# Two of eight tiles of the merged tensor, and two of 22 of the down projection's input, stored 64 bytes further up in a two-layer encoder kernel

## The chip, the core and the metric

The kernel runs on one core of a Trainium2 chip. The metric is the device time of one execution in microseconds. Before the change three runs took 911.18, 912.65 and 914.66 us; their median, 912.65 us, is the time before.

## What is computed

Two layers on a sequence of 256 tokens with 1024 features, all in float32, then a final norm. Each layer is

```python
h = rmsnorm(x);  p = h @ w_in                     # 1024 x 6672
o_dn = gated_delta_rule(...both directions)       # 512 features
o_hg = hgrn2_scan(...both directions)             # 512 features
merged = sigmoid(g_dn) * (o_dn @ w_branch_dn) + sigmoid(g_hg) * (o_hg @ w_branch_hg)
x = x + merged @ w_out                            # 1024 x 1024
h = rmsnorm(x);  gate, up = split(h @ w_up)       # 1024 x 2 * 2816
x = x + (silu(dwconv(gate) + bias) * up) @ w_down # 2816 x 1024
```

The change concerns `merged`, the input of `w_out`, and the input of `w_down`.

## The kernel before

Features lie on the 128 partitions, tokens along the free axis, so an activation of 1024 features is eight tiles of 128 x 256 (`KT = 8`, `T = 256`), and the down projection's input is 22 (`NF`). A large product is made from two roundings to `float32r`: a high part and the remainder, of the weights (`wh`, `wl`, made at L217 and L218 from a 128 x 1024 piece of raw weights that SP's queue has loaded) and of the activations (`xh`/`xl`, `mhi`/`mlo`, `hh`/`hl`, made by `split_act`, L278 to L281). For each 128 x 128 block of weights and each tile `k` of the activation TensorE does three products into one PSUM tile: `wh` with the high part, `wh` with the low part, `wl` with the high part (`Gemm.run`, all recorded at L149). The weights are the stationary operand, loaded anew for every product; the activation tile, 256 columns, is the moving one. A product is named in the profile by output, moving operand, stationary operand: `ps<-mhi,wh`. In a few of the input projections (`tokens=True`) the roles are turned: there the weights move and the activation is stationary (`ps<-wh,xh`).

A column pair is 256 output features, two PSUM halves (`m`). So per column pair there are 3 products x 2 halves x the number of tiles: 48 for eight tiles, 132 for 22.

The end of a layer, the part that matters here, goes in this order:

- `branches` (L940): the two branch products; their sum, gated, is split tile by tile into `mhi` and `mlo`, eight tiles of 256 columns each, kept in one tile of SBUF apiece.
- `project`: four column pairs with `w_out`, 4 x 48 = 192 products. The last tiles, `k` = 6 and 7, come out of `branches` last, and the scheduler lets some products of the second column pair go ahead of them.
- `ffn` (L1000 on): 22 column pairs with `w_up`, 22 x 48 = 1056 products on `xh`/`xl`; each gives one tile `j` of the down projection's input, split into `hh` and `hl` (tags `h0`, `l0`, `h1`, ...), each its own SBUF tile.
- then four column pairs with `w_down`, 4 x 132 = 528 products over `j` = 0 to 21. In the first layer products for the next layer (`ps<-xw,early`) stand between them, in the second, at the start of the third and the fourth column pair, three transposes (`pt`, L1129).

The order on every engine is set by the framework's scheduler, from the order of the calls and the priorities in `OPT["order"]`. Nothing in the second half of the layer is looped at run time.

Where tiles lie is partly chosen by hand. `placed` pads a tile by 64 elements (256 bytes) and starts it `shift` elements in:

```python
t_ = pool.tile([P, n + 64], dtype, **kw)[:, shift:shift + n]
```

In the built program every moving operand of the float32r products whose weights are stationary (`ohl`, `mhi`, `mlo`, `xh`, `xl`, `hh`, `hl`, `sas`) starts 192 bytes above a multiple of 256, and every stationary block of weights at a multiple of 256. In the turned products it is the reverse: moving at 0, stationary at 192. This text calls the remainder modulo 256 bytes an operand's **phase**.

Of the kernel before, what the change touches and what calls it, by code (L numbers as in the profile page):

```python
# [11 lines left out]
F32R = mybir.dt.float32r  # L12
# [5 lines left out]
P = 128  # L18
T = 256
D = 1024  # L20
KT = 8
# [6 lines left out]
OPT = {  # L28
    "f32": ((1, 4, 5, 6, 14), (1, 4, 5, 6, 14)),
    "hb": 1,  # L30
    "pad": 2,
    "obb": 2,
    "kcb": 2,
    "ahead": 2000,
    "raw": 3,
    "w": 3,
# [82 lines left out]
def trunk(ctx: ExitStack, tc: tile.TileContext, x_in, consts, masks, vec, rows, w16, w_in, w_br, w_out, w_up, w_down, out):  # L119
# [46 lines left out]
    for c in range(4):  # L166
        t_ = xp.tile([P, 2 * T + 2], F32, tag=f"x{c}", name=f"x{c}")
# [20 lines left out]
    def placed(pool, dtype, shape, shift, **kw):  # L188


        n = math.prod(shape)
        t_ = pool.tile([P, n + 64], dtype, **kw)[:, shift:shift + n]
        if len(shape) == 2:
            return t_.rearrange("p (a b) -> p a b", a=shape[0])
        return t_.rearrange("p (a b c) -> p a b c", a=shape[0], b=shape[1])

    def tmp(name, tag="tmp"):
        return tp.tile([P, 512], F32, tag=tag, name=name, bufs=OPT[tag])
# [6 lines left out]
    def split_piece(src, n):  # L205
        with tc.high_priority(offset=OPT["ahead"]):
            return split_piece_(src, n)
# [51 lines left out]
    def gemm(src, xh, xl, nk=KT, tokens=False, tail=0, parts=None):  # L259
        return Gemm(src, xh, xl, nk, tokens, tail, parts).run()  # L260
# [17 lines left out]
    def split_act(src, hi, lo):  # L278
        act.copy(hi, src)
        dve.tensor_tensor(lo, src, hi.bitcast(F32), ALU.subtract)  # L280
        return hi, lo  # L281
# [117 lines left out]
    def mixer(l, pre, rs):  # L399
        V = vecs[:, l]  # L400
        with ExitStack() as mc:
            mp = mc.enter_context(tc.tile_pool(name=f"mp{l}", bufs=1, reuse_waits=OPT["rw"]))
# [46 lines left out]
            for k0 in range(0, KT, 4):  # L449
# [3 lines left out]
                hi = xp.tile([P, 4, T], F32R, tag=f"xh{k0}", name="xh")  # L453
                lo = xp.tile([P, 4, T], F32R, tag=f"xl{k0}", name="xl")
# [8 lines left out]
            cb = mp.tile([P, 2, 8, P], F32, tag="cb", name="cb")  # L463
# [47 lines left out]
            qk = mp.tile([P, 2, H, T], F32, tag="qk", name="qk")  # L511
# [386 lines left out]
            hl = {}  # L898
# [41 lines left out]
            def branches():  # L940
                oh = [hl[i][0][:, h] for i in range(2) for h in range(H)]
                ol = [hl[i][1][:, h] for i in range(2) for h in range(H)]
                mhi = placed(mp, F32R, (KT, T), OPT["at"][l][1], tag="qk", name="mhi")
                mlo = placed(mp, F32R, (KT, T), OPT["at"][l][1], tag="cb", name="mlo")
                for c in range(4):
                    pb = [pg.tile([P, 512], F32, tag="g", name="pbr") for _ in range(2)]
                    gs = [Group(24) for _ in range(2)]
                    for i in range(2):
                        wh, wl = split_piece(w_br[l, c, i], 1024)
                        for kk in range(4):  # L950
                            a, b_ = oh[4 * i + kk], ol[4 * i + kk]
                            for m in range(2):
                                o = pb[m][:, i * T:(i + 1) * T]
                                whm, wlm = wh[:, kk, m * P:(m + 1) * P], wl[:, kk, m * P:(m + 1) * P]
                                gs[m].mm(o, whm, a)
                                gs[m].mm(o, whm, b_)
                                gs[m].mm(o, wlm, a)
                    for m in range(2):
                        tm = tmp("mg")
                        dve.tensor_tensor(tm, pb[m], sgs[0][:, 2 * c + m].rearrange("p a b -> p (a b)"), ALU.mult)  # L960
                        dve.tensor_tensor(tm[:, 0:T], tm[:, 0:T], tm[:, T:512], ALU.add)
                        a, b_ = split_act(tm[:, 0:T], mhi[:, 2 * c + m], mlo[:, 2 * c + m])
                        mh.append(a)
                        ml.append(b_)

# [2 lines left out]
            def project():  # L968
                rs, xs = Rms(), SplitX(V[:, V_FFN:V_FFN + 8])
                up = Gemm(lambda i: w_up[l, 0, i], xs.h, xs.l)  # L970
                for c in range(4):
                    if c == 3 and OPT["eu"]:
# [7 lines left out]
            stages = {"gs": gatesums, "k0": lambda: conv(2), "k1": lambda: conv(3),  # L980
                      "ks": kstats, "qs": qstats, "vt": vtok, "de": decay, "gn": lambda: gram(0), "gp": lambda: gram(1), "so": solve, "in": inverse,
                      "dl": delta, "do": dnout, "br": branches, "pr": project}
            for i, c in enumerate((0, 1, 4, 5)):
                stages[("q0", "q1", "v0", "v1")[i]] = lambda c=c: conv(c)
# [17 lines left out]
    def ffn(l, rs, xs, first):  # L1002
        V = vecs[:, l]
        last = l == OPT["layers"] - 1
        with tc.tile_pool(name=f"fp{l}", bufs=1, reuse_waits=OPT["rw"]) as fp:

            def early(src):
                t_ = fp.tile([P, 1024], F32, tag="early", name="early", bufs=2 * len(PRE))
                sp.dma_start(t_, src)
                return t_  # L1010

            hh, hl = [], []
            for j in range(NF):
                ps = gemm(lambda i: w_up[l, j, i], xs.h, xs.l) if j else first.run()
                if j == 0:
                    rb = rs.spread(fp)
                pad = fp.tile([P, T + 2], F32, tag="fpad", name="fpad", bufs=3)
                pool.memset(pad[:, 0:1], 0.0)
                pool.memset(pad[:, T + 1:T + 2], 0.0)
                dve.tensor_tensor(pad[:, 1:T + 1], ps[:, 0:T], rb, ALU.mult)  # L1020
                up = fp.tile([P, T], F32, tag="up", name="up", bufs=3)
                dve.tensor_tensor(up, ps[:, T:512], rb, ALU.mult)
                w = V[:, V_FCONV + 3 * j:V_FCONV + 3 * j + 3]
                cv = fp.tile([P, T], F32, tag="cv", name="cv", bufs=3)
                act.activation(cv, pad[:, 0:T], AF.Identity, scale=w[:, 0:1], bias=V[:, V_FBIAS + j:V_FBIAS + j + 1])
                for i in (1, 2):
                    dve.scalar_tensor_tensor(cv, pad[:, i:i + T], w[:, i:i + 1], cv, op0=ALU.mult, op1=ALU.add)  # L1027
                sl = fp.tile([P, T], F32, tag="sl", name="sl", bufs=3)
                act.activation(sl, cv, AF.Silu)
                dve.tensor_tensor(up, up, sl, ALU.mult)  # L1030
                hi = fp.tile([P, T], F32R, tag=f"h{j}", name="hh")
                lo = fp.tile([P, T], F32R, tag=f"l{j}", name="hl")
                a, b = split_act(up, hi, lo)
                hh.append(a)
                hl.append(b)
            rs = Rms()
            pre = None if last else Pre(l + 1, early)
            for c in range(4):
                if c == 3 and not last:
                    with tc.high_priority(offset=OPT["ep"]):  # L1040
                        todo = pre_order(6)
                        pre.mm(todo[:OPT["ek"]])
                if c == OPT["ec"] and not last:
                    pre.ahead(l + 1)
                gm = Gemm(lambda i: w_down[l, c, i] if i < 5 else w_down[l, c, i][:, 0:512], hh, hl, NF,
                          tail=OPT["mt"] if c == 3 else 0)
                ps = gm.run()
                parts = 2 if c == 3 and OPT["mt"] else 1
                for i in range(0, 2, 2 // parts):
                    s = slice(i, i + 2 // parts)  # L1050
                    dve.tensor_tensor(xx2[c][:, s], xx2[c][:, s], ps.rearrange("p (a b) -> p a b", a=2)[:, s], ALU.add)
                if not last:
                    pre.add(c)
                rs.add(c, parts)
                if last:
                    for k in (2 * c, 2 * c + 1):
                        act.activation(x[k], x[k], AF.Identity, scale=V[:, V_FIN + k:V_FIN + k + 1])
            if not last:
                if OPT["pc"]:
                    pre.last = gm.g.prev  # L1060
                rest = todo[OPT["ek"]:] + [(j, k) for j in range(len(PRE)) for k in (6, 7)]
                rs, _ = meet(pre, rs, rest, OPT["fa"])
        return pre, rs

    def pre_order(n):
        return [(j, k) for j in range(len(PRE)) for k in range(n)]

    def meet(pre, rs, todo, n):

        pre.mm(todo[:n])  # L1070
        rm, rs = rs, rs.finish(pre.last if n else None)
        pre.mm(todo[n:], rm.last)
        return rs, rm
# [62 lines left out]
    for i in range(4):  # L1136
        h, b = divmod(i, 2)
        o = op.tile([P, 4 * P], F32, tag="o", name="o")
# [85 lines left out]
```

## Time and profile before

| what | value |
|---|---|
| runs before | 911.18, 912.65, 914.66 us, median 912.65 |
| the profiled execution | 911.13 us |
| its span, first to last instruction | 909.0 us |
| TensorE busy (PE) | 888.8 us, 98% of the span |
| weight loads (PEld) | 869.6 us, 96% |
| VectorE (DVE), ScalarE (ACT) | 670.6 us (74%), 559.5 us (62%) |
| mean granted TensorE clock | 0.993 |

The profiled execution took 2.1 us more than its span, for what lies around it. Busy time of PE is a union of overlapping products: one product is recorded as some 280 ns long while the next starts within 120 ns. How fast the engine goes is therefore read from the distance between the starts of neighbouring products, and from how many fall into a stretch. In a table of stretches the number behind the x counts every product under way in the stretch, the two or three that reach over its edges too.

### The profile page before, as it was taken

The page shows a single profiled execution, that of the slowest core. Times are in us where ns is not written, and L with a number is a line of the kernel's source. Part 1 is how long each engine was busy: PE and PEld are TensorE (multiplying, and loading weights), DVE is VectorE, ACT ScalarE, POOL GpSimd, SP SyncE. Part 2 cuts the span into 40 slices and gives each one's busy share as a digit, 9 for nine tenths or more (in the row PEclk, how much of TensorE's full clock was granted, in tenths as well). Part 3 has the DMA queues.
Part 4 walks back from the last instruction along what each step waited for, and adds up shares of the span by engine and source line. Part 5 has one row for each costly group of instructions (what it writes and reads, how often), then busy time and mean ns, then how long its engine had stood idle before and what let it go on. Part 6 is the DMA issues. An engine that isn't in the chain of part 4 may idle for free.

```text
span 909.0 us, 18703 instructions
## 1 busy us (share of the span) xinstructions
PE 888.8 (98%) x7438; PEld 869.6 (96%) x7438; DVE 670.6 (74%) x1279; ACT 559.5 (62%) x972; POOL 13.9 (2%) x123
## 2 busy tenths in 40 slices
PE   6999999999999999999999999999999999999997
PEld 5988999999999999999988899999999999999996
DVE  5668897755877888865436789986568798888543
ACT  4698657678566655544425867474774776566443
POOL 0000000000000000000000000000000000000000
PEclk9999999999999999999998999999999999999998
DMA  6455565225667656655413565542256656666562
GB/s 213 135 188 168 172 187 139 65 76 174 191 187 262 202 187 189 188 175 185 152 50 119 183 199 168 168 118 82 84 180 202 195 188 195 199 190 196 179 192 81
DMA packets 51111, 150.07 MB, mean 165 GB/s; under 512 B 13488, under 2 KB 14032, under 8 KB 50768
## 3 DMA queue, kind: packets, MB, share of 16 engines
q1 hardware_dynamic: 50304, 147.96, 52.3%
q8 instruction: 58, 0.95, 0.4%
q10 hardware_dynamic: 720, 0.92, 0.3%
q14 instruction: 29, 0.24, 0.1%
HBM read 146.75 MB, written 2.11 MB: 164 GB/s over the span
## 4 chain that ended last, share of the span: by engine, by line
PE 88%; ACT 4%; DVE 3%; DMA 3%; issue 1%; SPq 0%; DVEq 0%; ACTq 0%
PE ps L149 72%; PE pbr L149 5%; PE pa L857 3%; DMA raw<-in_w_in_dram 2%; DVE wl L218 1%; DMA ld<-dg 1%; PE psb L149 1%; PE po L149 1%; PE poh L149 1%; ACT wh L217 1%; DVE pr L654 1%; DVE xs L656 1%; PE pz L693 0%; PE pr L716 0%; PE pz L712 0%
## 5 line engine op out<-in xcount | busy, mean ns | idle before, releaser
L217 ACT CAST wh<-raw 128x1024 fp32r<-128x1024 f32 x244 | 252.4, 1037 | 241.2 <-PE ps L149 121.6
L218 DVE TENSOR_TENSOR wl<-raw,wh 128x1024 fp32r<-128x1024 f32 x244 | 293.4, 1204 | 120.8 <-ACT wh L217 117.8
L149 PE MATMUL ps<-xh,wh 128*128 128x256 f32 x1152 | 322.3, 281 | 1.3 <-ACT wh L217 1.3
L149 PE MATMUL ps<-xh,wl 128*128 128x256 f32 x1152 | 322.0, 281 | 1.5 <-DVE wl L218 1.5
L149 PE MATMUL ps<-xl,wh 128*128 128x256 f32 x1152 | 321.1, 280 | 0.0
L149 PEld LDWEIGHTS ps<-xh,wl 128*128 128x128 f32 x1152 | 217.5, 189 | 2.3 <-DVE wl L218 2.2
L149 PEld LDWEIGHTS ps<-xh,wh 128*128 128x128 f32 x1152 | 216.1, 188 | 1.7 <-ACT wh L217 1.5
L149 PEld LDWEIGHTS ps<-xl,wh 128*128 128x128 f32 x1152 | 216.1, 188 | 0.1
L149 PE MATMUL ps<-hl,wh 128*128 128x256 f32 x352 | 98.6, 280 | 0.0
L149 PE MATMUL ps<-hh,wl 128*128 128x256 f32 x352 | 98.6, 280 | 0.0
L149 PE MATMUL ps<-hh,wh 128*128 128x256 f32 x352 | 98.3, 279 | 0.0
L149 PEld LDWEIGHTS ps<-hh,wl 128*128 128x128 f32 x352 | 66.6, 189 | 0.1
L149 PEld LDWEIGHTS ps<-hh,wh 128*128 128x128 f32 x352 | 66.3, 188 | 0.0
L149 PEld LDWEIGHTS ps<-hl,wh 128*128 128x128 f32 x352 | 66.2, 188 | 0.1
L149 PE MATMUL ps<-xnt,raw 128*128 128x256 f32 x256 | 61.4, 392 | 0.0
L149 PEld LDWEIGHTS ps<-xnt,raw 128*128 128x128 f32 x256 | 48.8, 198 | 6.6
L149 PE MATMUL ps<-wl,xh 128*128 128x256 f32 x160 | 46.7, 292 | 0.6 <-DVE wl L218 0.5
L149 PE MATMUL ps<-wh,xh 128*128 128x256 f32 x160 | 46.1, 289 | 0.2 <-ACT wh L217 0.2
L149 PE MATMUL ps<-wh,xl 128*128 128x256 f32 x160 | 45.6, 285 | 0.0
L1027 DVE SCALAR_TENSOR_TENSOR cv<-fpad,vecs,cv 128x256 f32<-128x256 f32 x88 | 42.0, 481 | 4.0
L149 PE MATMUL pbr<-ohl,wh 128*128 128x256 f32 x256 | 44.3, 278 | 0.0
L149 PEld LDWEIGHTS pbr<-ohl,wh 128*128 128x128 f32 x256 | 38.5, 189 | 0.0
(279 smaller groups left out, 1436.4 us busy)
## 6 DMA issues: line engine op xcount, KB each, us to landing
raw<-in_w_in_dram SPq DMA_DIRECT2D x99, 512.0 KB, 3.7
raw<-in_w_up_dram SPq DMA_DIRECT2D x88, 512.0 KB, 4.1
raw<-in_w_down_dram SPq DMA_DIRECT2D x40, 512.0 KB, 3.6
raw<-in_w_br_dram SPq DMA_DIRECT2D x16, 512.0 KB, 3.7
raw<-in_w_out_dram SPq DMA_DIRECT2D x16, 512.0 KB, 4.1
cb<-cd SPq DMA_DIRECT2D x2, 1024.0 KB, 5.1
early<-in_w_in_dram SPq DMA_DIRECT2D x4, 512.0 KB, 6.8
raw<-in_w_down_dram SPq DMA_DIRECT2D x8, 256.0 KB, 3.2
```

Of the source, the lines that this page charges most:

```text
L149: self.prev = chain(pe.matmul(o, lhsT, rhs, start=self.i == 0, stop=self.i == self.n - 1), self.prev)
L217: act.copy(wh[:, :n], raw[:, :n])
L218: dve.tensor_tensor(wl[:, :n], raw[:, :n], wh.bitcast(F32)[:, :n], ALU.subtract)
L654: dve.tensor_tensor(prv, view(lm[:, j + 1, j:j + 1], [[32, n], [0, w]]), view(xs[:, j, 0:1], [[0, n], [1, w]]), ALU.mult)
L656: dve.tensor_tensor(xs[:, j + 1:32, 0:w], xs[:, j + 1:32, 0:w], prv, ALU.subtract)
L857: pe.matmul(pa[:, u // 2, u % 2], kc[:, u * P:(u + 1) * P], view(qa[:, 0, u * P:u * P + 1], [[2 * h, 64 // h], [512 + h, 2], [1, h]]), sta ...
L1027: dve.scalar_tensor_tensor(cv, pad[:, i:i + T], w[:, i:i + 1], cv, op0=ALU.mult, op1=ALU.add)
```

## The change

```diff
-                mhi = placed(mp, F32R, (KT, T), OPT["at"][l][1], tag="qk", name="mhi")
-                mlo = placed(mp, F32R, (KT, T), OPT["at"][l][1], tag="cb", name="mlo")
+                mhi, mlo = [], []
+                for tag, name, m_ in (("qk", "mhi", mhi), ("cb", "mlo", mlo)):
+                    t_ = mp.tile([P, KT * T + 64], F32R, tag=tag, name=name)
+
+                    for k in range(KT):
+                        o = OPT["at"][l][1] + k * T + (16 if k >= KT - 2 else 0)
+                        m_.append(t_[:, o:o + T])
...
-                        a, b_ = split_act(tm[:, 0:T], mhi[:, 2 * c + m], mlo[:, 2 * c + m])
+                        a, b_ = split_act(tm[:, 0:T], mhi[2 * c + m], mlo[2 * c + m])
...
-                hi = fp.tile([P, T], F32R, tag=f"h{j}", name="hh")
-                lo = fp.tile([P, T], F32R, tag=f"l{j}", name="hl")
+                room, on = (64, 16) if j < 2 else (0, 0)
+                hi = fp.tile([P, T + room], F32R, tag=f"h{j}", name="hh")[:, on:on + T]
+                lo = fp.tile([P, T + room], F32R, tag=f"l{j}", name="hl")[:, on:on + T]
```

Sixteen elements are 64 bytes. Tiles 6 and 7 of `mhi` and `mlo`, and tiles 0 and 1 of `hh` and `hl`, now start at phase 0; all the others stay at 192. The four wider tiles move what lies above them in the pool `fp` by 256 to 1024 bytes, whole multiples of 256, so no other phase changes. The instructions, their order on each of the five engines, and what each waits for are the same as before; only addresses differ.

Per column pair 12 products (2 tiles x 2 halves x 3) have their moving operand at phase 0, with the stationary one at phase 0 too. In the order of the program they stand as follows, counted in products from the first on `mhi`, alike in both layers:

| stage | products at phase 192 (u) and at phase 0 (c), in order |
|---|---|
| `w_out`, 192 products | 38 u, 1 c, 12 u, 6 c, 11 u, 5 c, 11 u, 12 c, 36 u, 12 c, 36 u, 12 c |
| `w_up`, 1056 products | all u |
| `w_down`, 528 products | four times: 12 c, 120 u (with `early` products or `pt` transposes between some) |

## Rows read from the trace of the kernel before

**Rows 1.** The page: busy time, then the chain that ended last, by engine and by line.
```profile
PE 888.8 (98%) x7438; PEld 869.6 (96%) x7438; DVE 670.6 (74%) x1279; ACT 559.5 (62%) x972; POOL 13.9 (2%) x123
...
PE 88%; ACT 4%; DVE 3%; DMA 3%; issue 1%; SPq 0%; DVEq 0%; ACTq 0%
PE ps L149 72%; PE pbr L149 5%; PE pa L857 3%; DMA raw<-in_w_in_dram 2%; DVE wl L218 1%; DMA ld<-dg 1%; PE psb L149 1%; PE po L149 1%; PE poh L149 1%; ACT wh L217 1%; DVE pr L654 1%; DVE xs L656 1%; PE pz L693 0%; PE pr L716 0%; PE pz L712 0%
```

**Rows 2.** Stretches, PE: from:to us, length, busy (products), clock, DMA share, GB/s.
```profile
248.00:270.00 22.00, 22.00 (x190) 1.00 0.64 193
...
697.00:718.00 21.00, 21.00 (x188) 1.00 0.64 195
...
840.00:868.00 28.00, 28.00 (x249) 1.00 0.59 186
870.00:884.00 14.00, 14.00 (x122) 1.00 0.57 174
886.00:899.00 13.00, 13.00 (x117) 1.00 0.20 62
```

**Rows 3.** Timeline of PE, first layer, w_up: first and last of 189 successive products.
```profile
299.79 0.28 PE L149 MATMUL ps<-xh,wl 128*128 128x256 f32 x1
...
321.93 0.28 PE L149 MATMUL ps<-xl,wh 128*128 128x256 f32 x1
```

**Rows 4.** Timeline of PE, second layer, w_up: first and last of 188 successive products.
```profile
759.79 0.28 PE L149 MATMUL ps<-xl,wh 128*128 128x256 f32 x1
...
780.98 0.28 PE L149 MATMUL ps<-xh,wl 128*128 128x256 f32 x1
```

**Rows 5.** Timeline of PE, 583.0 to 585.1 us; 4, 4 and 7 products are left out.
```profile
583.02 0.28 PE L149 MATMUL ps<-xh,wh 128*128 128x256 f32 x1
...
583.58 0.28 PE L149 MATMUL ps<-wl,xh 128*128 128x256 f32 x1
...
584.15 0.28 PE L149 MATMUL ps<-xh,wl 128*128 128x256 f32 x1
...
585.10 0.28 PE L149 MATMUL ps<-xl,wh 128*128 128x256 f32 x1
```

**Rows 6.** Timeline of PE, 586.5 to 587.7 us; 6 products are left out.
```profile
586.58 0.28 PE L149 MATMUL ps<-xh,wh 128*128 128x256 f32 x1
586.70 0.28 PE L149 MATMUL ps<-wh,xh 128*128 128x256 f32 x1
586.81 0.28 PE L149 MATMUL ps<-xl,wh 128*128 128x256 f32 x1
...
587.64 0.28 PE L149 MATMUL ps<-xh,wl 128*128 128x256 f32 x1
```

**Rows 7.** Timeline of PE, 115.1 to 117.1 us; 5, 2 and 7 products are left out.
```profile
115.13 0.28 PE L149 MATMUL ps<-wh,xl 128*128 128x256 f32 x1
...
115.84 0.28 PE L149 MATMUL ps<-wh,xl 128*128 128x256 f32 x1
...
116.20 0.28 PE L149 MATMUL ps<-xh,wl 128*128 128x256 f32 x1
...
117.10 0.28 PE L149 MATMUL ps<-xl,wh 128*128 128x256 f32 x1
```

**Rows 8.** Timeline of PE, 576.3 to 577.8 us; 5 and 6 products are left out.
```profile
576.27 0.28 PE L149 MATMUL ps<-wh,xh 128*128 128x256 f32 x1
...
576.98 0.28 PE L149 MATMUL ps<-xh,wl 128*128 128x256 f32 x1
...
577.80 0.28 PE L149 MATMUL ps<-xh,wh 128*128 128x256 f32 x1
```

**Rows 9.** Timeline of PE: the two sets of transposes within the second layer's w_down.
```profile
869.04 0.49 PE L1129 MATMUL pt<-cst,x 128*128 128x128 f32 x3
...
884.92 0.49 PE L1129 MATMUL pt<-cst,x 128*128 128x128 f32 x3
```

## The prediction

> **What bounds the kernel.** I read the page first. TensorE is busy 98% of the span and stands for 88% of the chain that ended last, `ps` products at L149 alone for 72% [rows 1]. So a nanosecond added to or taken from every product of the long stages shows in the end time almost whole. The change adds and removes no instruction and no wait; it can act only through the pace of TensorE. I therefore looked at that pace stage by stage.
>
> There are **two paces**, a short and a long one. In the first layer's `w_up`, 188 successive starts lie 22.14 us apart, 117.8 ns each [rows 3]; in the second layer's `w_up`, the same instructions, 187 lie 21.19 us apart, 113.3 ns each [rows 4]. The difference is 4.45 ns per product, 3.9%. It is not the clock: the granted clock is 1.00, the 2.4 GHz level, in every stretch shown [rows 2]. It is not the operands' phases either, which are 192 for what moves and 0 for the weights in both layers, and not a wait, for the engine has no gap. A pace lasts: `w_out` of the first layer runs at 117 ns (22 us for 190 products, some 2.4 of them from the edges), `w_out` of the second at 113 ns, and both keep their pace to the end of `w_up` [rows 2 to 4]. In `w_down` of the second layer it changes twice: 249 products in 28 us before 868 us is the short pace, 122 in 14 us after 870 us the long, 117 in 13 us after 886 us the short again, and the changes come with the transposes at 869.04 and 884.92 us, which break the row of equal products [rows 2, 9]. The first set lengthened the pace, the second shortened it again. So: two paces, each of which holds itself, and a break in the pattern can throw the engine from one into the other.
>
> **What a change of phase does.** The trace has breaks of the kind that the change makes: where normal products and turned ones (moving operand at phase 0 in place of 192) follow each other without a gap.
>
> - From the short pace: at 583.02 us the engine keeps 112 ns; five products from 583.58, the turned ones, stay at 114 ns (0.57 us for five), and behind the return to phase 192 at 584.15 eight products take 0.95 us, 119 ns each, the long pace [rows 5]. A single turned product at 586.70 us does the same: seven products behind it take 0.83 us, 118.6 ns each, where the two starts around it had been 0.115 apart [rows 6].
> - From the long pace: six turned products from 115.13 us take 0.71 us (118 ns); four products after the return to 192 it is the short one, eight in 0.90 us, 112.5 ns [rows 7]. Elsewhere a return at the long pace keeps it: 118 ns before 576.98 us (six in 0.71), 117 ns behind (seven in 0.82) [rows 8].
>
> So a move up to phase 0 leaves the short pace as it is, the move back turns it into the long one, and only a phase-0 stretch at the long pace has been seen to end in the short one. The reservation: in all these places the weights' phase changes along with the moving operand's, whereas the change leaves the weights at 0. The trace has no run of products with both at 0 beyond the one product at such a border.
>
> **The change, term by term.**
>
> 1. *The second layer, phase-192 products.* They keep the short pace now. The first changed product stands after 38 of `w_out`, and the return behind it lengthens the pace as in [rows 6]. Behind it lie 12 + 11 + 11 + 36 + 36 = 106 products of `w_out` at phase 192, 1056 of `w_up` and 480 of `w_down`, 1642 in all. 120 of these are at the long pace already, the column pair between the two transposes [rows 2, 9]. 1522 x 4.45 ns = +6.8 us. Each later group of changed products repeats the throw, so nothing brings the short pace back for long.
> 2. *The first layer, phase-192 products.* Long before, long after: 0.
> 3. *The changed products themselves,* 2 layers x 8 column pairs x 12 = 192. Their price with both operands at 0 is not in the trace. The lower bound is the short pace, 113.3; the upper is the longest pace of any border in these rows, 119 ns [rows 5]. At the short pace the first layer's 96 gain 4.45 ns each, -0.4 us, and the second layer's 96 nothing; at 119 ns they cost 96 x 1.2 + 96 x 5.7 ns = +0.7 us. I take the short pace, since [rows 5] keeps it on moving up: -0.4 us.
> 4. *The splits that write the moved tiles, and DVE, ACT, SP:* the same instructions beside TensorE's 98%; 0. They stand 74% and 62% busy, and a slower TensorE gives them more room.
>
> Sum +6.4 us, bounds +6.4 to +7.5. On the profiled execution, 911.13 us, that is 917.5. The median of the runs shown is 1.5 us higher and the spread 3.5 us; the profile does not tell whether that lies in the mixers, which would add to the new time as well, or in stretches of the long pace that are now counted twice. I forecast **918.0 us**, a little over the sum; this case by itself reaches from 915.5 to 921.
>
> A rule speaks against all of this. The Trainium skill ("TensorE: Matmul & The Clock Gate", Part 2, the step on LDWEIGHTS) says that TensorE reads moving operand and weights through two independent ports, and that loading the next weights takes no read bandwidth from the running product. By that rule an operand's address would be of no matter and the time would stay as it is, the second rival below. The rows do not refute it for bandwidth, but they show two paces for one shape at one clock, which it does not foresee.
>
> **The rivals.**
>
> - *Thrown into the short pace.* The mechanism is the same border, the other outcome: the return from phase 0 to 192 brings the short pace, as at 116 us [rows 7]. It decides at the last return of `w_out`, before 1056 products without a break. Then the first layer gains 106 + 1056 + 480 + 96 products x 4.45 = 7.7 us and the second the 130 products between its transposes, 0.6 us: 911.1 - 8.3 = 902.8 us, faster. For it: the groups are so placed that one stands just ahead of `w_up`; a stretch of both-at-0 products at the long pace may end in the short one. Against it: each return from a phase-0 stretch at the short pace in [rows 5, 6] went to the long one. Chance 0.11.
> - *Nothing.* Either the moving operand's phase alone is of no effect (in the rows the weights' moved too, and may be the cause), or each group flips the pace and the flips cancel: six groups in `w_out` and four in `w_down` leave `w_up` of each layer as it is. By both the time stays within 1 us, 911 to 913. For it: the reservation above. Against it: a pace that outlasts the border from `w_out` to `w_up`, where no phase changes [rows 2 to 4], and is lost where one does [rows 5, 6]. Chance 0.20.
> - *One layer each way:* the first turns to the short pace, the second to the long: 911.1 - 7.7 + 6.4, some 910 us. Chance 0.04.
>
> **How the numbers follow.** The forecast has 0.65. The range from 911 to 921 us takes in its own range and the case of nothing, 0.85 together, and leaves out the first rival. A difference of 0.5% (4.6 us) is about what a measurement of this kernel tells from none. Of the forecast's 0.65 I count 0.57 as beyond it and 0.08 within, since the sum is only 1.8 us over that line; with nothing (0.20) and the mixed case (0.04) same has 0.32; faster has the first rival, 0.11.
>
> **What would show it.** In the profile after, `w_up` of both layers at 117.8 ns per product (281 ns recorded each, where the second layer now has 276); in the second layer the pace lengthens some 40 products into `w_out`; the runs of 12 changed products at 113 ns; the first layer until `w_out` unchanged; and a smaller spread among runs, since the pace behind `w_out` no longer depends on how it was entered. Wrong: `w_up` of the first layer at 113 ns, or the second still there. If the changed products stand at neither pace, term 3 is at fault.

## The result: faster, by the throw that was forecast the other way

The changed kernel takes **905.45 us**, the median of four runs (904.76, 905.39, 905.52, 908.29), against 912.59 for four runs of the kernel before; the ratio is 0.9935, 0.65% less, with a 95% interval from 0.9917 to 0.9952. Run again later beside experiments it took 904.53 us (0.9938, 0.9918 to 0.9958). The forecast was 918.0, in a range from 911 to 921. The profiled execution took 904.76 us, with a span of 902.6 against 909.0.

First the page of the changed kernel: busy time, and the chain that ended last by engine. They answer to [rows 1].

```profile
PE 881.7 (98%) x7438; PEld 862.7 (96%) x7438; DVE 670.3 (74%) x1279; ACT 559.9 (62%) x972; POOL 14.0 (2%) x123
...
PE 85%; ACT 5%; DMA 5%; DVE 3%; issue 1%; SPq 0%; DVEq 0%; ACTq 0%
```

The same instructions, TensorE as busy as before, 7.1 us less of it. So the gain lies in the pace, and the stretches tell where. Of the kernel before one stretch, in `w_up` of the first layer (PE: from:to us, length, busy (products), clock, DMA share, GB/s):

```profile
282.00:390.00 108.00, 108.00 (x919) 1.00 0.62 192
```

Stretches of the changed kernel: `w_up` of the first and of the second layer, then `w_down` of the second before, between and behind the two sets of transposes.

```profile
282.00:390.00 108.00, 108.00 (x956) 1.00 0.63 200
...
724.00:832.00 108.00, 108.00 (x956) 1.00 0.63 196
840.00:862.00 22.00, 22.00 (x196) 1.00 0.63 196
864.00:878.00 14.00, 14.00 (x125) 1.00 0.59 179
880.00:893.00 13.00, 13.00 (x117) 1.00 0.20 62
```

Take off the 2.4 products that reach over the edges, and 919 in 108 us is 117.8 ns each, the long pace of [rows 3]; 956 is 113.3, the short pace of [rows 4]. **The first layer went over to the short pace, and the second stayed in it.** The 14 us between the transposes, 122 products in [rows 2], now hold 125: short too, but for the last products of a changed group at their start. The granted clock is 1.00, the 2.4 GHz level, in all of them.

How much of the 6.4 us of span lies in the end of each layer is read from the first product on `mhi` and the last on `hh`. In the timeline of PE of the kernel before:

```profile
247.85 0.28 PE L149 MATMUL ps<-mhi,wh 128*128 128x256 f32 x1
...
462.56 0.28 PE L149 MATMUL ps<-hh,wl 128*128 128x256 f32 x1
...
697.00 0.28 PE L149 MATMUL ps<-mhi,wh 128*128 128x256 f32 x1
...
899.89 0.28 PE L149 MATMUL ps<-hh,wl 128*128 128x256 f32 x1
```

and in that of the changed kernel:

```profile
248.92 0.28 PE L149 MATMUL ps<-mhi,wh 128*128 128x256 f32 x1
...
457.43 0.28 PE L149 MATMUL ps<-hh,wl 128*128 128x256 f32 x1
...
690.55 0.28 PE L149 MATMUL ps<-mhi,wh 128*128 128x256 f32 x1
...
893.49 0.28 PE L149 MATMUL ps<-hh,wl 128*128 128x256 f32 x1
```

The end of the first layer went from 214.71 to 208.51 us, -6.20; that of the second from 202.89 to 202.94, +0.05. Ahead of the first the changed kernel is 1.07 us later, between the two 1.32 shorter, behind the second equal (9.11). The four add up to -6.40. The two numbers outside the ends don't belong to the change: in the twelve traces below the first product on `mhi` starts between 247.5 and 249.1 us, and the piece between the ends takes from 231.5 to 236.7 us, without following what was edited, whereas the ends repeat: the changed kernel's second trace gives 208.52 and 202.94. Part of the scatter between the ends is the granted clock just behind the first end: with moving 0 and weights 64 it is 1.00 from 455 to 500 us (the shortest piece, 231.5), with moving at 128 it is 0.86 from 455 to 475 and 0.91 from 475 to 500, partly at the 1.2 GHz level (the longest, 236.7); TensorE is busy 18.96 us of the first 20 in both. The experiments are therefore read by these two lengths as well as by their times.

Now one group of twelve changed products in `w_out` of the first layer, timeline of PE of the changed kernel. The group is the twelve starts from 264.24 to 265.54; 4, 6, 3, 2 and 4 rows are left out.

```profile
263.67 0.28 PE L149 MATMUL ps<-mlo,wh 128*128 128x256 f32 x1
...
264.24 0.28 PE L149 MATMUL ps<-mhi,wh 128*128 128x256 f32 x1
...
265.06 0.28 PE L149 MATMUL ps<-mlo,wh 128*128 128x256 f32 x1
...
265.54 0.28 PE L149 MATMUL ps<-mhi,wl 128*128 128x256 f32 x1
265.66 0.29 PE L149 MATMUL ps<-mhi,wh 128*128 128x256 f32 x1
...
266.02 0.28 PE L149 MATMUL ps<-mhi,wh 128*128 128x256 f32 x1
...
266.59 0.28 PE L149 MATMUL ps<-mhi,wl 128*128 128x256 f32 x1
```

Five products before it take 0.57 us, 114 ns each. The first seven of the group take 0.82, 117 each; the next four 0.48, 120 each: neither pace. Three products after the return the pace is 114 again (five in 0.57). Behind every changed group of five and more, in both layers, the pace is the short one within five products, whatever stood ahead: the long pace at 440 us, the short one at most others, `early` products or transposes at some. Within a group, where no `early` products or transposes cut it, the starts lie 112 to 124 ns apart. In `w_out` of the first layer the lone first product, at 253.39 us, had already ended the long pace. A group of twelve with the four products behind it takes 74 to 80 ns more than 16 at the short pace, by the starts in the trace.

### The profile page after: what moved, and what is told of

Read it like the earlier page. It is cut to its first block, busy times and chain, and to the rows that moved or that the text cites. A ratio compares the mean times of both kernels' runs of the same rounds, so it can differ in the third digit from the quotient of the medians.

```text
span 902.6 us, 18703 instructions
## 1 busy us (share of the span) xinstructions
PE 881.7 (98%) x7438; PEld 862.7 (96%) x7438; DVE 670.3 (74%) x1279; ACT 559.9 (62%) x972; POOL 14.0 (2%) x123
## 4 chain that ended last, share of the span: by engine, by line
PE 85%; ACT 5%; DMA 5%; DVE 3%; issue 1%; SPq 0%; DVEq 0%; ACTq 0%
PE ps L149 69%; PE pbr L149 5%; PE pa L857 3%; DMA raw<-in_w_in_dram 3%; DVE wl L218 1%; ACT wh L217 1%; PE po L149 1%; DMA ld<-dg 1%; PE poh L149 1%; PE psb L149 1%; ACT cacc L527 1%; PE pz L693 0%; PE pr L716 0%; DVE cacc L534 0%; PE pz L712 0%
## 5 line engine op out<-in xcount | busy, mean ns | idle before, releaser
L149 PE MATMUL ps<-xnt,raw 128*128 128x256 f32 x256 | 58.9, 381 | 0.5 <-ACT srk L573 0.5
```

The source lines that it names most:

```text
L149: self.prev = chain(pe.matmul(o, lhsT, rhs, start=self.i == 0, stop=self.i == self.n - 1), self.prev)
```

## The experiments

**The theory** after the result: a stretch of products with both operands at phase 0 has a pace of its own, near 120 ns, and puts TensorE into the short pace when it ends, whatever the pace before. The turned products, on which the prediction rested, have moving 0 and stationary 192; the difference is the weights' phase. **Rivals:** a border throws either way, and the first layer's turn was chance; or the weights' phase is no matter.

The table has all twelve, with time, ratio to the kernel before (run beside each, 910.72 to 910.85 us), and the two lengths (first layer's end, second layer's; before: 214.71 and 202.89). The edits further down are written in short form, against the changed kernel unless it is said otherwise; the phases that they give are those of the kernels that ran, and the order of the products is the same in all.

| kernel | us | ratio [95%] | first end | second end |
|---|---|---|---|---|
| only `mhi`, `mlo` | 905.51 | 0.9954 [0.9932, 0.9975] | 208.87 | 203.23 |
| only `hh`, `hl` | 909.08 | 0.9989 [0.9976, 1.0003] | 213.57 | 202.59 |
| single products | 905.90 | 0.9950 [0.9932, 0.9969] | 208.62 | 203.20 |
| phases of the turned products | 911.19 | 1.0002 [0.9991, 1.0013] | 214.40 | 203.34 |
| moving at 64 | 904.85 | 0.9952 [0.9925, 0.9979] | 208.51 | 203.95 |
| moving at 128 | 906.33 | 0.9950 [0.9930, 0.9970] | 208.59 | 203.05 |
| moving 0, weights 64 | 902.30 | one run | 208.49 | 203.22 |
| weights alone at 64 | 904.83 | one run | 208.47 | 203.21 |
| last group as turned | 916.77 | 1.0066 [1.0047, 1.0084] | 214.31 | 209.04 |
| all of `w_out` both at 0 | 905.68 | one run | 209.27 | 204.16 |
| groups of six | 903.43 | 0.9919 [0.9902, 0.9937] | 208.01 | 203.18 |
| the change again | 904.53 | 0.9938 [0.9918, 0.9958] | 208.52 | 202.94 |

### Each half alone

The edit for the first: `hh` and `hl` as before the change.

```diff
-                room, on = (64, 16) if j < 2 else (0, 0)
+                room, on = 0, 0
```

Expected: 

> Only tiles 6 and 7 of mhi and mlo are moved; hh and hl stay at phase 192. Theory (a stretch with both operands at phase 0 has a pace of its own near 118 to 120 ns, and every return from it to phase 192 is to the short pace, whatever the pace before): the first layer's w_up at 113.3 ns per product as in the changed kernel, its w_down short up to the first early products and long behind them; the second layer's w_up at 113.3, and the 120 products between its transposes long as before. Worked out from the two traces: w_out with w_up of the first layer -4.9 us, its w_down -1.2, the second layer's six groups +0.3: 5.8 us less than before, some 907 us. Rival (a border throws the pace either way, and the first layer's turn in the changed kernel was a matter of where it happened to stand): w_up of one layer or of both at 117.8 ns, 910 to 917 us.

The second leaves `mhi` and `mlo` as they were:

```diff
-                        o = OPT["at"][l][1] + k * T + (16 if k >= KT - 2 else 0)
+                        o = OPT["at"][l][1] + k * T
```

Expected: 

> Only tiles 0 and 1 of hh and hl are moved; mhi and mlo stay at phase 192. Theory: the first layer's w_out and w_up stay at 117.8 ns as before; w_down of both layers is short behind each of its groups, but for what follows early products; the stretch between the transposes of the second layer turns short. From the two traces: w_down of the first layer -1.4 us, of the second -0.3: some 911 us. Rival (the throw of the first layer comes from elsewhere, for instance from addresses in the pool, or any change of phase does it later): w_up of the first layer at 113.3 ns, 905 to 907 us, or w_down as before and 912.6 us.

Both came out by the theory. The merged tensor's half brings 5.84 us in the first layer's end and costs 0.34 in the second's; the down projection's brings 1.14 and 0.30. With the second alone the first layer's `w_up` has 919 products in the 108 us from 282 us, as before the change; with the first alone, 953 in 107.92. So the large part of the gain hangs on the last group ahead of `w_up`, and the groups in `w_down` only reach what follows them. Behind the `early` products the pace is long in every one of these kernels until the next group.

### Single products

```diff
-                        o = OPT["at"][l][1] + k * T + (16 if k >= KT - 2 else 0)
+                        o = OPT["at"][l][1] + k * T + (16 if (k, name) == (7, "mlo") else 0)
...
-                room, on = (64, 16) if j < 2 else (0, 0)
+                oh_, ol_ = 0, 16 if j == 0 else 0
...
```

(`oh_` and `ol_` then take the place of `on` for `hi` and `lo`.)

Expected: 

> Only tile 7 of mlo and tile 0 of hl are moved: 32 changed products in place of 192, each alone between two products at phase 192. Theory with one product as good as twelve (the lone changed product at 253.9 us, after which the pace was short): everything as in the changed kernel, w_up of both layers at 113.3 ns. In the changed kernel's trace a group of twelve takes 80 ns more than 16 products at the short pace would with the four behind it, a lone one 26 to 29: per layer 346 + 320 ns for its groups against 16 x 27 = 432 ns here, 0.5 us less for two layers: some 905 us, within 0.5 us of the changed kernel. Rival (a stretch is needed, one product is not enough): the first layer's w_up at 117.8 ns, 910 to 912 us.

The time fits the theory, but "one product as good as twelve" does not hold. Timeline of PE of this kernel; the changed products are at 256.84 and 257.20, then at 259.55 and 259.90:

```profile
256.84 0.28 PE L149 MATMUL ps<-mlo,wh 128*128 128x256 f32 x1
...
257.20 0.28 PE L149 MATMUL ps<-mlo,wh 128*128 128x256 f32 x1
...
257.43 0.28 PE L149 MATMUL ps<-mlo,wh 128*128 128x256 f32 x1
...
259.44 0.28 PE L149 MATMUL ps<-mhi,wh 128*128 128x256 f32 x1
...
260.62 0.28 PE L149 MATMUL ps<-mlo,wh 128*128 128x256 f32 x1
...
261.98 0.28 PE L149 MATMUL ps<-mlo,wh 128*128 128x256 f32 x1
```

Behind the first pair 17 products take 2.01 us, 118 ns each: still long. Behind the second, 12 take 1.36, 113 each. The next column pairs leave it short. A pair met the long pace again at 440 us, and there too it stayed long. A lone product resets sometimes; here it was in time for `w_up`.

### The phases of the turned products in the same place

Moving operand of the same twelve products at phase 0 as in the change, but their weights read 48 elements further up, at phase 192 (`hh` and `hl` as before the change):

```diff
+                        if self.up and k >= 6:
+                            whm, wlm = (bass.AP(tensor=w_.tensor, offset=w_.offset + self.up - (P if (k, m) == (7, 1) else 0),
+                                                ap=[list(d) for d in w_.ap]) for w_ in (whm, wlm))
...
-                    ps = gemm(lambda i: w_out[l, c, i], mh, ml)
+                    ps = gemm(lambda i: w_out[l, c, i], mh, ml, up=48)
```

Expected: 

> As with only tiles 6 and 7 of mhi and mlo moved, but their weights in w_out are read 192 bytes further up, at phase 192, so that these products have the phases of the turned ones (moving 0, stationary 192). The last block of 128 columns is read twice in place of its neighbour, so w_out computes with some wrong weights; the number of products and the instructions are unchanged. Theory (the weights' phase decides: both at 0 resets to the short pace, 0 with 192 keeps the pace and the return lengthens it, as the prediction had read from the turned products): the groups run at 113 or 118 ns, w_up of the second layer at 117.8 ns, +4.7 us there and up to +2.1 in w_down before the transposes; the first layer long or short; between 912 and 921 us. Rival (the moving operand's phase alone is what matters): as with the weights at 0, both w_up at 113.3 ns, some 907 us.

The rival fell: the weights' phase counts. Timeline of PE, the last two groups of the first layer's `w_out`, from 263.72 and from 269.23 us:

```profile
263.72 0.28 PE L149 MATMUL ps<-mhi,wh 128*128 128x256 f32 x1
...
265.02 0.28 PE L149 MATMUL ps<-mhi,wl 128*128 128x256 f32 x1
...
265.60 0.28 PE L149 MATMUL ps<-mlo,wh 128*128 128x256 f32 x1
...
266.50 0.28 PE L149 MATMUL ps<-mhi,wh 128*128 128x256 f32 x1
...
269.23 0.28 PE L149 MATMUL ps<-mhi,wh 128*128 128x256 f32 x1
...
270.47 0.28 PE L149 MATMUL ps<-mhi,wl 128*128 128x256 f32 x1
...
270.82 0.28 PE L149 MATMUL ps<-xh,wl 128*128 128x256 f32 x1
...
271.88 0.28 PE L149 MATMUL ps<-xh,wl 128*128 128x256 f32 x1
```

The first group keeps the long pace (eleven starts in 1.30 us, 118 ns) and leaves the short one behind it (eight in 0.90, 112.5). The second keeps the short pace (eleven in 1.24, 113) and leaves the long one (nine in 1.06, 118). **With these phases every border turns the pace over**: all six groups of either layer did. Six turns give back the pace on entry, so `w_up` was long in the first layer and short in the second, as before, and the time is that of the kernel before. My expectation of a long second layer was wrong, since I had not counted the turns.

### The last group alone with the turned phases

Against the kernel before this one:

```diff
-                    ps = gemm(lambda i: w_out[l, c, i], mh, ml, up=48)
+                    ps = gemm(lambda i: w_out[l, c, i], mh, ml, up=48 if c == 3 else 0)
```

Expected: 

> As with tiles 6 and 7 of mhi and mlo moved (hh and hl stay), but in the last column pair of w_out alone their weights are read 192 bytes further up: the first five groups have both operands at phase 0, the last twelve products before w_up have 0 and 192 (the last block of weights is read twice in place of its neighbour: some wrong weights in that column pair). Theory (both at 0 resets to the short pace; 0 with 192 keeps the short pace and its return lengthens it): w_up of BOTH layers at 117.8 ns per product. First layer as before the change; second layer +4.7 us in w_up, +1.2 in w_down up to the first transposes, up to 0.6 less between the transposes: 5.3 to 6 us more than before, some 916 to 917 us. Rival (the groups before, or the number of breaks, decide, and the last group changes nothing): w_up of both layers at 113.3 as with tiles 6 and 7 of mhi and mlo moved alone, some 905 us.

916.77 us, with both layers at the long pace. Timeline of PE, the last group of the first layer (twelve starts from 268.32 to 269.57) and what follows:

```profile
268.32 0.28 PE L149 MATMUL ps<-mhi,wh 128*128 128x256 f32 x1
...
269.57 0.28 PE L149 MATMUL ps<-mhi,wl 128*128 128x256 f32 x1
...
269.92 0.28 PE L149 MATMUL ps<-xh,wl 128*128 128x256 f32 x1
...
271.45 0.28 PE L149 MATMUL ps<-xh,wh 128*128 128x256 f32 x1
```

Eleven at 114 ns, then 13 starts in 1.53 us, 117.7. Stretches of the same kernel, `w_up` of the first and of the second layer:

```profile
282.00:390.00 108.00, 108.00 (x919) 1.00 0.60 190
...
724.00:830.00 106.00, 106.00 (x902) 1.00 0.60 185
```

The second layer's has 902 products in 106 us, where all the other kernels have 937 or 938. Its end took 6.15 us more than before, just over the 5.3 to 6 expected. Twelve products in each layer, of 7438 in all, move the time by 11 us, from 905.51 (the same tiles with all weights at 0) to 916.77, by the phase of their weights alone. That shows the cause: the last border ahead of `w_up` sets the pace of what follows, and for a group of twelve the pair of phases sets what the border does.

### Other phases

The moving operand 128 and 192 bytes up in place of 64 (in `mhi` and `mlo` tiles 6 and 7 then lie ahead of the other six, since there is no room above):

```diff
-                        o = OPT["at"][l][1] + k * T + (16 if k >= KT - 2 else 0)
+                        o = OPT["at"][l][1] + k * T + (-1536 - 32 if k >= KT - 2 else 512)
...
-                room, on = (64, 16) if j < 2 else (0, 0)
+                room, on = (64, 32) if j < 2 else (0, 0)
```

(-16 and 48 in the second). Expected at phase 64: 

> The same tiles as in the change, moved 128 bytes up in place of 64: moving operand at phase 64, weights at 0. Theory (what counts is the difference between the phase of the operand that moves and that of the weights that are loaded beside it; the normal products have 192, both at 0 have 0, the turned ones 64): a difference of 64, as in the turned products, so the groups run at either pace as these do, 113.3 or 117.8 ns, and not at the 118 to 120 ns of both at 0, and the return throws from one pace into the other: six groups in w_out leave w_up as it was, long in the first layer, short in the second, 909 to 913 us. Rival (any step of phase with the weights at 0 resets to the short pace): w_up of both layers at 113.3 ns, 904 to 907 us.

Expected at phase 128: 

> The same tiles moved 192 bytes up: moving operand at phase 128, weights at 0, a difference of 128 that no product has yet had in these traces. Theory of the difference: alike in the pace of the groups and in the throw to the run with the weights alone moved by 64 (192 with 64, the same difference), whichever it is. Bounds from the four cases seen: all short 904 to 907 us; nothing 909 to 913; the second layer thrown long 915 to 919. Rival (any step of phase with the weights at 0 resets): w_up of both layers at 113.3 ns, 904 to 907 us.

Weights and moving operand both 64 bytes up (the tiles of the change), and the weights alone (`mhi` and `mlo` as before the change); both with `hh` and `hl` as before and, against the kernel with the phases of the turned products,

```diff
-                    ps = gemm(lambda i: w_out[l, c, i], mh, ml, up=48)
+                    ps = gemm(lambda i: w_out[l, c, i], mh, ml, up=16)
```

Expected with both moved: 

> Tiles 6 and 7 of mhi and mlo at phase 0 and their weights in w_out at 64: both moved by 64, the difference stays 192. The last block of weights is read twice in place of its neighbour, so w_out computes with some wrong weights. Theory of the difference: inside a group the products run at the pace that they had before it, 113.3 or 117.8 ns, and not at 118 to 120; only the two edges of a group can throw. Rival (the moving operand at phase 0 is what is slow and resets): 118 to 120 ns inside each group and the short pace behind it, as in the changed kernel, w_up of both layers at 113.3.

Expected for the weights alone: 

> All moving operands at phase 192 as before; only the weights of tiles 6 and 7 in w_out are read 64 bytes further up, at phase 64 (the last block twice in place of its neighbour: some wrong weights). Theory of the difference: 128, so pace and throw as with the moving operand at phase 128 and the weights at 0. Rival (the address of the weights is of no matter): nothing changes, no border is seen, w_up at 117.8 ns in the first layer and 113.3 in the second, as before.

In all four both layers' `w_up` follows the last twelve products of `w_out` at the short pace: 955 products from 282 to 390 us in the first. The times, 902.30 to 906.33 us, went with that, where the theory of the difference had 909 to 913 for moving at 64. The address of the weights matters with the moving operand untouched, so that rival fell. The theory of the difference holds in part. Right: a difference of 128 runs in the same pattern of starts from either side (115, 118, 122, 120 and 119 ns in turn); differences of 64 and 192 run at 117.8 ns and not at the 120 of both at 0. Wrong: neither of the latter keeps the short pace, which the turned products (64) and the normal ones (192) do. The timeline of PE with the moving operand at 64, group from 263.64 to 264.94:

```profile
263.64 0.28 PE L149 MATMUL ps<-mhi,wh 128*128 128x256 f32 x1
...
265.05 0.28 PE L149 MATMUL ps<-mhi,wh 128*128 128x256 f32 x1
...
265.40 0.28 PE L149 MATMUL ps<-mhi,wh 128*128 128x256 f32 x1
...
265.97 0.28 PE L149 MATMUL ps<-mhi,wl 128*128 128x256 f32 x1
```

Entered at the short pace, the twelve take 1.41 us, 117.5 ns each; behind, five take 0.57, 114. So both phases count, each for itself. Nor is the short return a rule for these: with the moving operand at 64 the groups of one, five and six products in `w_out`, and those cut by `early` products or transposes, left the long pace behind; with the weights alone at 64 the group of five did, in both layers; at 128 the group behind the first `early` products did. Both at 0 reset from five products on in every instance. Moving 0 with weights at 64 left the short pace behind all its groups too, but of these only the first, a single product, had met the long pace.

### All of `w_out` with both at 0

```diff
-                        o = OPT["at"][l][1] + k * T + (16 if k >= KT - 2 else 0)
+                        o = OPT["at"][l][1] + k * T + 16
```

(`hh` and `hl` as before the change.) Expected: 

> All eight tiles of mhi and mlo at phase 0, hh and hl as before: all 192 products of w_out of each layer have both operands at phase 0. The steady pace of such products, the price of the third term: theory 119 to 120 ns (as in the second half of the groups of twelve), so w_out takes 192 x 120 = 23.0 us in both layers against 22.6 and 21.8 before; and one return, at the end of w_out, to the short pace: w_up at 113.3 ns in both layers. Rival (118 to 120 ns is the price of the edges, and a long stretch falls back to 113.3 or 117.8): w_out 21.8 or 22.6 us.

The steady price, which no trace had shown. Stretches of this kernel within `w_out` of the first and of the second layer:

```profile
250.00:271.00 21.00, 21.00 (x177) 1.00 0.62 182
691.00:713.00 22.00, 22.00 (x185) 1.00 0.63 191
```

177 less 2.4 in 21 us is 120.3 ns; single starts lie at 120 almost without exception. It does not fall back to either pace, and both layers' `w_up` follow at the short one (956 products from 282 to 390 us, 937 from 724 to 830). The 192 products take 23.03 and 23.02 us, as expected, 120.0 ns each.

### Fewer changed products, and the change again

Tile 7 alone, tile 0 alone, and in the first layer tile 6 of `hh` and `hl`, which comes behind the `early` products:

```diff
-                        o = OPT["at"][l][1] + k * T + (16 if k >= KT - 2 else 0)
+                        o = OPT["at"][l][1] + k * T + (16 if k == 7 else 0)
...
-                room, on = (64, 16) if j < 2 else (0, 0)
+                room, on = (64, 16) if j == 0 or (l, j) == (0, 6) else (0, 0)
```

Expected: 

> Half of the groups and one more place: only tile 7 of mhi and mlo, tile 0 of hh and hl, and in the first layer tile 6 of hh and hl too (behind the early products, where the changed kernel runs at the long pace). Groups of six in place of twelve. Theory: a group of six resets as well (the groups of five and six in w_out of the changed kernel did), for 40 ns in place of 80: 20 groups, 0.8 us less; and the 181 long products behind the early ones in the first layer's w_down mostly short, 0.6 us less net: some 1.4 us below the changed kernel, 904 us. Rival (six are too few): long pace behind some of the groups, above all in w_down, 906 to 912 us.

The change itself, once more: 

> The changed kernel again, beside the others on the same chip: 905 us, w_up of both layers at 113.3 ns per product and 12 products each group at 118 to 120, as in its first trace. A rival to every account that makes the return to the short pace a rule: if it is chance, one of the layers' w_up stands at 117.8 here, and the time is 909 to 917 us.

The change repeats to 0.01 us in both ends. The groups of six cost 40 ns each, as expected, and reset wherever all six stand together; cut to four by the first transposes, a group left 125 products of the second layer long again (cut by the second ones, it left them short), and that gave back half of what the first layer gained: -0.50 us in the first end, +0.24 in the second, against the change. The median is 1.1 us lower, of which the two ends make 0.26, and the intervals of the ratios overlap: it beats the kernel before, and is not shown to beat the change.

## Why the prediction was wrong

The step that failed is the path of the pace behind a changed group: the prediction took the return from a group to phase 192 to lengthen the pace, as behind the turned products, and the runs show the short pace behind every group with both operands at 0: -6.20 us in the first layer's end and +0.05 in the second's, where the sum had 0 and about +6.4. Both signs of being wrong that the prediction names came up: `w_up` of the first layer at 113 ns, and changed products at neither pace.

- **What bounds the kernel:** right. TensorE stayed busy 98% of the span, and the time followed the pace of the products on `ps`. That the pace is held without a break through 1056 products, and can be lost where the phase changes, is what the experiments show again and again; the case of "nothing" fell with it, though turns that cancel do appear with the turned phases (911.19 us). The Trainium skill's page "TensorE: Matmul & The Clock Gate", Part 2, the step on LDWEIGHTS, has two independent read ports, one for the moving operand and one for the weights. That an address is of no matter was my inference from it, not the page's statement; here the weights' address alone moved the pace, and the measurement decides.
- **Term 3, the changed products at the short pace: failed.** I took it from [rows 5], where the weights lie at 192. Both at 0 runs at 120.0 ns in a steady stretch, above the upper bound of 119 that the rows gave. The reservation named this (no run of both at 0 in the trace), but I let it weigh 0.20, and for "nothing" only. In time the term is small: 346 ns of surcharge over the short pace in `w_out` and 320 in `w_down` of each layer, 1.3 us in all, worked out from the starts, against the -0.4 us forecast.
- **Term 1, the second layer thrown into the long pace, +6.8 us: failed, by the same step.** "The return behind it lengthens the pace as in [rows 6]" carried a border with the weights at 192 over to weights at 0. Measured: behind each group the short pace came back within five products; the 120 between the transposes became short instead of staying long. The second end came to +0.05 us: +0.33 in `w_out`, where the groups cost, and -0.28 in what follows, where the transposes' long stretch ends. With the turned phases at the last border the forecast's case does appear: 916.77 us, +6.15 in the second end.
- **Term 2, the first layer stays long: failed.** Of its products at phase 192, those behind the first changed one are short, but for 181 behind the `early` products; -6.20 us in the end of that layer.
- **Term 4:** right. VectorE and ScalarE were busy 670.3 and 559.9 us, against 670.6 and 559.5.
- **The first rival,** "thrown into the short pace", was the true one, with its place (the last return of `w_out`) and very nearly its price: 902.8 forecast against 904.76. It lacks the 181 long products behind the `early` ones, some 0.8 us, and the surcharge of the groups in both layers. It had 0.11 because I counted the two returns at the short pace in [rows 5, 6] against it and a single one for it. Both kinds are one behaviour, the turning over seen with the turned phases, and said nothing on a border of another kind. Two readings of the prediction are off, without bearing on its sum: in [rows 7] the short pace begins with the third product behind the return, not behind the fourth, and this rival counts 130 products between the transposes where term 1 counts 120.
- **The spread among runs** was to become smaller; it is 3.5 us in four runs, as before. Some of it lies between the ends of the layers, by the traces. Whether the pace behind `w_out` comes out alike in every execution is not shown, since one execution of each kernel was traced, and two of the changed one: with `mhi` and `mlo` alone twelve runs took 904.08 to 912.57 us, and with single products runs at the same mean clock, 0.996 over the whole kernel, took 905.36 and 910.93. A `w_up` at the long pace would add 1056 x 4.45 ns = 4.7 us (an estimate from [rows 3, 4]).

## What to carry to other kernels

Where a long row of equal products runs at two paces in two places at the same clock, look at the address phases of both operands at the last change ahead of it: some ten products at another phase can set the pace of a thousand. A border in the trace is a precedent only for the same pair of phases, moving and stationary; where the pair itself does not occur, the outcome is open in sign, and the range must hold both.

## What was not expected of the hardware

- One product of 128x128 with 256 columns, its weights loaded anew, at a granted clock of 1.00, starts every 113.3 or 117.8 ns with moving 192 and stationary 0, every 113 or 118 with 0 and 192, every 120 with 0 and 0, every 117.8 with 64 and 0 or 0 and 64, and every 118 to 119 with a difference of 128.
- The transposes in the second layer's `w_down` turn the pace over like the turned products: short, long, short in [rows 2, 9]; long, short, long where the last group had the turned phases (128 products from 875 us at 113.3 ns, 128 from 890 at 117.8).
- The return that stayed long in [rows 8], and another in the same trace at 572.32 us behind 13 turned products, do not fit the turning over. Why, and what within the engine or the memory makes the paces, stays open; the traces show the starts alone. Phases were moved in steps of 64 bytes only, and that the remainder has to be taken of 256 was not tested by itself; in the built program `xh` and `xl` lie at the same remainder even of 1024 bytes in both layers of the kernel before, where `w_up` ran at two paces.
